# Front of a streaming encoder step: two more feature shifts summed by VectorE, late rows scaled by GpSimd and ScalarE, two jobs one place later

## The chip, the core and the metric

The kernel runs on one core of one Trainium2 chip. A core has TensorE (matrix products, PE in the profile, with PEld for its weight loads), VectorE (DVE), ScalarE (ACT), GpSimd (POOL) and SyncE (SP), which here issues nearly all transfers. Each engine works through its own queue in order, and engines wait for each other by semaphores. The metric is the device time of one execution in microseconds (us), lower is better.

## The reference

One layer of a hybrid encoder for 1024 prompt frames and 32 sample frames. The change lies in the first lines, the modulated norm and the input projection:

```python
mod = jax.nn.silu(c) @ w_ada + b_ada
sh1, sc1, gt1, sh2, sc2, gt2 = jnp.split(mod[:, None, :], 6, axis=-1)

h = rmsnorm(x, g_mix) * (1 + sc1) + sh1
u = h @ w_in
qa, ka, va, qm, km, vm, om, ip, fp, ga, gm = jnp.split(u, _split_points(), axis=-1)
```

`c` has one row for the prompt and one for the sample, so every feature has two scales and two shifts. After it come band attention over `qa, ka, va`, a matrix memory over `qm, km, vm`, gates, an output projection, and a SwiGLU network. All inputs are float32.

## The kernel before

**Layout.** Activations lie transposed: 1024 features in eight groups of 128 partitions ("features 0 to 7", index `k` or `j`), and 1056 token columns (1024 prompt, then 32 sample). The columns are worked in three tiles of 352. `CUT` is 704: tiles 0 and 1 are the *early* columns, tile 2 the *late* ones, and only the late tile has sample columns (its last 32).

**Precision.** A float32 product is made of three passes: high half of the weights by high half of the activations, low by high, high by low (`PASSES`). For each feature ScalarE writes the high half of `h` (`high_h`), and VectorE the low half (`low_h`).

**Order.** Engines PE, ACT, DVE and POOL run exactly in the order in which the code records their instructions. `first_units` is the opening of the kernel, written out by hand:

1. `load_ada(n)` fetches the halves of the modulation weights in order; `n = 2j` is the scale of feature `j`, `n = 2j + 1` its shift. `ada_sums(j, part, pt)` makes both on TensorE with eight products of 128x128 each, and `ada_done` turns them into `s1` and `sh1` on ScalarE. For feature 7 the shift is not made so: its weights lie with the 1024 inputs along a row, and `shift_sum` has VectorE multiply them with a broadcast copy of silu(c) (`silb`) and add up, once for the prompt (`c` = 0) and once for the sample (`c` = 1).
2. Squares of the early columns are summed, `token_roots` and `powers` (GpSimd) make the inverse roots, `spread` has TensorE transpose them over all partitions, and ScalarE copies them to `RB`.
3. `scaled_x` multiplies the columns by scale and root, `high_h` adds the shift. TensorE takes the early columns of the first key, value and query blocks: `products(k, q)` is pass `q` of feature `k`, six matmuls. The loop over `k` from 1 to 7 prepares feature `k + 2` on VectorE and ScalarE beside it. Within it the squares of the late columns are made, summed on TensorE (`token_sums`, at `k` = 3), rooted, spread (at `k` = 4), and from `k` = 5 on `late_h` prepares the late columns, one step of one feature at a time: `scaled_x(k)`, `high_h(k - 1)`, `low_h(k - 2)`.
4. After `k` = 7 ScalarE and VectorE empty the early results (`put_k`, `put_v`, `put_q`), while TensorE runs the 48 late products into the bank `psS`.

In the late columns the prompt part (320 columns) and the sample part (32) go different ways before the change: VectorE scales and subtracts the 320, GpSimd the 32.

**Behind the opening.** `unit` is the general product of a block and a tile; while it runs, it takes one job at a time out of `side.later`: transposes of values (`v_tail`, TensorE L694), the split of cached keys (`cache_keys`, ScalarE L769, VectorE L771) and of cached values (`cache_values`, VectorE L684 and L685). Attention then starts: VectorE L828 (scores and their maximum), ScalarE L829, TensorE L841 (transposes), ScalarE L848 and VectorE L853 (their two halves), TensorE L873.

## Time and profile before

| | |
|---|---|
| median of three runs | 1589.97 us (1589.28 to 1590.21) |
| profiled execution: its own time | 1588.91 us |
| its span, first to last instruction | 1587.2 us |
| granted TensorE clock, mean | 0.998 |
| busy: PE, PEld, DVE, ACT, POOL | 99%, 98%, 70%, 50%, 26% |
| end of the opening (last late product) | 70.7 us after the start |

The profiled execution takes 1.7 us more than its span, and 1.06 us less than the median. In rows of the timeline the first number is the start in us after the span's start, the second the duration of the row's instructions together; then come engine, line, operation, the tiles written and read, the shape and the count. The bracket tells how long the engine sat idle before it and what ended that. In rows of waits stand the total, the number of times and the longest.

### The profile page before, as it was taken

Reading aid. Unit: us, or ns where it says so; the run is one execution under the profiler, and the core shown is the slowest. Engines: PE = TensorE matmul, PEld = TensorE weight load, DVE = VectorE, ACT = ScalarE, POOL = GpSimd, SP = SyncE. Lnnn points to the kernel's source line nnn. Section 1 sums busy time; section 2 is a strip of 40 time slices with the busy share of each in tenths; the row PEclk is TensorE's granted clock in tenths of the full one; section 3 lists DMA queues with packets and bytes.
Section 4 is the critical chain, followed back from the end, with each engine's and each line's share of the span. In section 5 each row is a group of like instructions: output and inputs, shape, how many; then the busy total and the mean of one; then the engine's idle time right before and its main releaser. Section 6 shows DMA issues by size and latency. Waiting matters only on the chain.

```text
span 1587.2 us, 27275 instructions
## 1 busy us (share of the span) xinstructions
PE 1564.9 (99%) x10181; PEld 1547.8 (98%) x10181; DVE 1107.6 (70%) x2282; ACT 788.5 (50%) x1742; POOL 420.5 (26%) x438
## 2 busy tenths in 40 slices
PE   8999999999999999999999999999999999999997
PEld 8999999999999999999999999999999999999997
DVE  3865655556767845446655699898888986799755
ACT  4765554544555545444434656544545444545443
POOL 0433343442222410000012100665665750000000
PEclk9999999999999999999999999999999999999999
DMA  9422233243132423584353312223222227427444
GB/s 374 138 66 82 88 104 99 92 133 105 42 91 74 86 82 104 115 288 162 108 156 113 94 55 67 82 73 102 68 89 87 68 87 251 137 80 252 129 136 156
DMA packets 176481, 187.08 MB, mean 118 GB/s; under 512 B 11766, under 2 KB 141466, under 8 KB 176222
## 3 DMA queue, kind: packets, MB, share of 16 engines
q1 hardware_dynamic: 173686, 183.50, 36.7%
q10 hardware_dynamic: 2664, 1.85, 0.4%
q8 instruction: 80, 1.31, 0.4%
q14 instruction: 51, 0.42, 0.1%
HBM read 151.15 MB, written 34.17 MB: 117 GB/s over the span
## 4 chain that ended last, share of the span: by engine, by line
PE 92%; DVE 3%; ACT 2%; issue 2%; POOL 1%; DMA 0%; ACTq 0%; POOLq 0%; DVEq 0%
PE mm L418 41%; PE psb L1889 18%; PE mm L1889 11%; PE psb L2271 3%; PE mm L968 3%; PE mm L2271 2%; PE psV L873 2%; PE psb L2135 2%; PE psS L814 2%; PE mm L329 2%; PE psT L841 1%; PE mm L2135 1%; PE psV L1202 1%; PE psT L1204 1%; PE psT L1199 1%
## 5 line engine op out<-in xcount | busy, mean ns | idle before, releaser
L418 PE MATMUL mm<-s,wsp 128*128 128x352 f32 x4104 | 686.9, 324 | 0.1
L418 PEld LDWEIGHTS mm<-s,wsp 128*128 128x128 f32 x4104 | 657.1, 188 | 1.8 <-issue 0.4
L381 DVE TENSOR_TENSOR wsp<-wraw,wsp 128x512 fp32r<-128x512 f32 (+1 forms) x280 | 235.6, 859 | 113.7 <-ACT wsp L380 111.9
L1889 PE MATMUL psb<-s,wsp 128*128 128x352 f32 x1611 | 271.7, 322 | 1.5 <-DVE wsp L381 0.8
L380 ACT ACTIVATE wsp<-wraw 128x512 fp32r<-128x512 f32 x336 | 199.6, 617 | 141.5 <-PE psb L1889 43.8
L1889 PEld LDWEIGHTS psb<-s,wsp 128*128 128x128 f32 x1611 | 260.5, 188 | 2.1 <-DVE wsp L381 1.1
L1889 PE MATMUL mm<-s,wsp 128*128 128x352 f32 x933 | 159.3, 322 | 0.0
L1889 PEld LDWEIGHTS mm<-s,wsp 128*128 128x128 f32 x933 | 151.2, 188 | 0.5 <-DVE wsp L381 0.5
L834 POOL TENSOR_SCALAR st<-st,mx 128x640 f32<-128x640 f32 (+5 forms) x72 | 53.3, 740 | 183.6 <-DVE mx L833 165.6
L1295 DVE CUSTOM_DVE_ANT_0 junk<-wa,t 128x512 bf16<-128x512 f32 x128 | 94.8, 741 | 3.4 <-DMA wa<-in_w_mod_dram 2.3
L381 POOL TENSOR_TENSOR wsp<-wraw,wsp 128x512 fp32r<-128x512 f32 x56 | 74.9, 1358 | 52.6 <-ACT wsp L380 50.3
L828 DVE CUSTOM_DVE_ANT_0 st<-psS,bias 128x640 f32<-128x640 f32 (+5 forms) x72 | 44.5, 618 | 57.5 <-PE psS L814 43.5
L829 ACT ACTIVATE st<-st,mx 128x640 f32<-128x640 f32 (+5 forms) x72 | 47.9, 666 | 64.1 <-DVE mx L828 63.9
L1836 POOL TENSOR_TENSOR t<-t,sl 128x352 f32<-128x352 f32 x19 | 18.4, 967 | 212.7 <-ACT sl L1834 212.7
L848 ACT ACTIVATE pT<-psT 128x640 fp32r<-128x640 f32 (+3 forms) x80 | 38.6, 493 | 64.5 <-PE psT L841 50.1
L2244 POOL TENSOR_TENSOR fst<-fst,mhalf 128x6 f32<-128x6 f32 x1 | 2.3, 2312 | 221.1 <-DVE fst L2243 221.1
L853 DVE TENSOR_TENSOR pT<-psT,pT 128x640 fp32r<-128x640 f32 (+3 forms) x80 | 44.0, 558 | 21.5 <-ACT pT L848 21.4
L1508 POOL TENSOR_TENSOR wraw<-wraw,raw 128x512 f32<-128x512 f32 x33 | 55.8, 1704 | 0.9
L968 PE MATMUL mm<-s,s 128*128 128x264 f32 (+3 forms) x432 | 54.5, 283 | 0.0
L2271 PE MATMUL psb<-s,wsp 128*128 128x352 f32 x330 | 54.2, 324 | 0.0
L2271 PEld LDWEIGHTS psb<-s,wsp 128*128 128x128 f32 x330 | 53.1, 188 | 0.1
L968 PEld LDWEIGHTS mm<-s,s 128*128 128x128 f32 (+1 forms) x432 | 51.9, 179 | 0.5
(376 smaller groups left out, 2460.6 us busy)
## 6 DMA issues: line engine op xcount, KB each, us to landing
wraw<-in_w_in_dram SPq DMA_DIRECT2D x37, 512.0 KB, 3.7
wraw<-in_w_gate_up_dram SPq DMA_DIRECT2D x33, 512.0 KB, 3.9
wa<-in_w_mod_dram SPq DMA_DIRECT2D x64, 256.0 KB, 2.8
wraw<-in_w_down_dram SPq DMA_DIRECT2D x32, 512.0 KB, 4.3
a_d<-t SPq DMA_DIRECT2D x22, 528.0 KB, 2.8
g_d<-t SPq DMA_DIRECT2D x16, 528.0 KB, 3.4
t<-g_d SPq DMA_DIRECT2D x16, 528.0 KB, 4.8
s<-in_w_ada_dram SPq DMA_DIRECT2D x16, 512.0 KB, 8.0
```

Source lines behind the costliest of these rows:

```text
L380: act.activation(dst[:, 0], src, AF.Copy)
L381: eng.tensor_tensor(dst[:, 1], src, f(dst[:, 0]), op=ALU.subtract)
L418: pe.matmul(pt[:, :hi - lo], wt[(w0 + k) // 4][:, a, (w0 + k) % 4], xt[k][:, b, lo:hi], start=(k == 0 and q == 0), stop=(k == n - 1 and q ...
L828: dve.tensor_tensor_reduce(so, sv, bi, -1.0, 3.0e38, ALU.add, ALU.min, mx[:n, 1:2])
L829: act.activation(st[:n, :w], st[:n, :w], AF.Exp, bias=mx[:n, 1:2], scale=-1.0, accum_out=mx[:n, 2:3])
L834: pool.tensor_scalar(st[:n, :w], st[:n, :w], mx[:n, 3:4], 1.0, op0=ALU.mult, op1=ALU.mult)
L968: pe.matmul(pt[:n, :wd], hs[k][:, a, i * P:i * P + n], whl[b][:, k, :wd], start=(k == 0 and q == 0), stop=(k == KD - 1 and q == 2))
L1295: dve.tensor_tensor_reduce(junk, wa, crow[:, c], 1.0, 0.0, ALU.mult, ALU.add, at)
L1508: self.eng.tensor_tensor(a(dst), a(x), a(y), op=op)
L1889: pe.matmul(acc, wt[:, a, k], x[k][:, b], start=(start and not onto and k == 0 and q == 0), stop=(stop and k == 3 and q == 2), skip_group_ ...
L2135: pe.matmul(acc, wt[k // 4][:, u, k % 4], piece_of[k, i][:, v], start=(k == 0 and q == 0), stop=(k == KP - 1 and q == 2))
L2271: pe.matmul(acc, wt[(k - k0) // 4][:, u, (k - k0) % 4], piece_of[k, 2][:, v], start=(k == 0 and q == 0), stop=(k == NF - 1 and q == 2))
```

## The change

- `load_ada(13)`, the shift weights of feature 6, is fetched behind `silb` instead of ahead of the late columns of x; the host lays the shift weights of feature 6 out as those of feature 7.
- `ada_sums(6, 1)` on TensorE is gone. VectorE makes the shifts of feature 6 with two calls of `shift_sum`, so there are four in the loop, at `k` = 2, 4, 5 and 6, behind the `late_h` steps of their `k`.
- `ada_sums(7, 0)` stands ahead of the first products instead of behind their first pass; both `ada_done` stand earlier on ScalarE.
- The power of the early roots is taken in two instructions of three columns instead of one of six.
- The late columns of a feature are one piece of 352 for GpSimd (times `RB`), two for ScalarE (320 and 32, with scale and shift of their part, then one copy of 352 to the high half), and one of 352 for VectorE (the low half).
- The spread of the late roots stands behind `products(4, 2)`, and `cache_values` one place later among the side jobs.

```diff
     def load_ada(n):
         j, i = divmod(n, 2)
-        if i == 0:
+        if j == len(was):
             was.append(slot([P, 2, D]))
...
     load_first(0)
-    load_ada(13)
     load_ada(14)
...
-    def powers(t0, t1):
-        x = roots[:, :, 3 * t0:3 * t1]
-        pool.tensor_tensor(x[:, 1], x[:, 0], mhalf[:, :3 * (t1 - t0)], op=ALU.pow)
+    def powers(t):
+        x = roots[:, :, 3 * t:3 * t + 3]
+        pool.tensor_tensor(x[:, 1], x[:, 0], mhalf[:, :3], op=ALU.pow)
...
     def scaled_x(j, lo, hi):
-        for c, a, b in col_segments(lo, hi):
-            x = xTs[j][:, a:b]
-            if c == 0:
-                dve.scalar_tensor_tensor(x, x, s1[:, 0, j:j + 1], RB[:, a:b], op0=ALU.mult, op1=ALU.mult)
-            else:
-                pool.tensor_tensor(x, x, RB[:, a:b], op=ALU.mult)
+        x = xTs[j][:, lo:hi]
+        if hi <= CUT:
+            dve.scalar_tensor_tensor(x, x, s1[:, 0, j:j + 1], RB[:, lo:hi], op0=ALU.mult, op1=ALU.mult)
+        else:
+            pool.tensor_tensor(x, x, RB[:, lo:hi], op=ALU.mult)
 
     def high_h(j, lo, hi):
         if lo == 0:
             hs.append(slot([P, 2, T], F32R))
+        x, h = xTs[j][:, lo:hi], hs[j][:, 0, lo:hi]
+        if hi <= CUT:
+            act.activation(h, x, AF.Identity, bias=sh1[:, 0, j:j + 1])
+            return
         for c, a, b in col_segments(lo, hi):
-            x, h = xTs[j][:, a:b], hs[j][:, 0, a:b]
-            if c == 0:
-                act.activation(h, x, AF.Identity, bias=sh1[:, 0, j:j + 1])
-            else:
-                act.activation(x, x, AF.Identity, scale=s1[:, 1, j:j + 1], bias=sh1[:, 1, j:j + 1])
-                act.activation(h, x, AF.Copy)
+            o = xTs[j][:, a:b]
+            act.activation(o, o, AF.Identity, scale=s1[:, c, j:j + 1], bias=sh1[:, c, j:j + 1])
+        act.activation(h, x, AF.Copy)
 
     def low_h(j, lo, hi):
-        for c, a, b in col_segments(lo, hi):
-            x, o, h = xTs[j][:, a:b], hs[j][:, 1, a:b], f(hs[j][:, 0, a:b])
-            if c == 0:
-                dve.scalar_tensor_tensor(o, x, sh1[:, 0, j:j + 1], h, op0=ALU.add, op1=ALU.subtract)
-            else:
-                pool.tensor_tensor(o, x, h, op=ALU.subtract)
+        x, o, h = xTs[j][:, lo:hi], hs[j][:, 1, lo:hi], f(hs[j][:, 0, lo:hi])
+        if hi <= CUT:
+            dve.scalar_tensor_tensor(o, x, sh1[:, 0, j:j + 1], h, op0=ALU.add, op1=ALU.subtract)
+        else:
+            dve.tensor_tensor(o, x, h, op=ALU.subtract)
...
         sp.dma_start(silb, bass.AP(sil_d.tensor, sil_d.offset, [[0, P], [D, 2], [1, D]]))
+        load_ada(13)
         load_ada(15)
...
         spread(1)
-        ada_sums(6, 1, pt)
+        ada_done(6, pt)
+        ada_sums(7, 0, psS)
         for t in range(2):
             scaled_x(0, *early[t])
             high_h(0, *early[t])
-        ada_done(6, pt)
+        ada_done(7, psS)
...
             for i in range(3):
                 product(0, i, 0, t)
-        ada_sums(7, 0, psS)
         scaled_x(1, 0, CUT)
...
-            if k in (3, 4):
-                shift_sum(7, k - 3, silb)
+            for i in {5: (0, 1, 2), 6: (3, 4), 7: (5, 6)}.get(k, ()):
+                late_h(i)
+            for j, c in {2: [(6, 0)], 4: [(7, 0)], 5: [(6, 1)], 6: [(7, 1)]}.get(k, ()):
+                shift_sum(j, c, silb)
+            products(k, 2)
             if k == 4:
                 for i, n in enumerate((P, P, NT - 2 * P)):
                     pe.transpose(tok[:, i * P:i * P + n], roots[:n, 1, 6 + i:7 + i].to_broadcast([n, P]), ident[:n, :n])
                 act.activation(RB[:, late[0]:late[1]], tok[:, :NT], AF.Copy)
-            for i in {5: (0, 1, 2), 6: (3, 4), 7: (5, 6)}.get(k, ()):
-                late_h(i)
-            products(k, 2)
...
-                side.later += [lambda: cache_keys(early_loads[0]), nothing, lambda: cache_values(early_loads[0])]
+                side.later += [lambda: cache_keys(early_loads[0]), nothing, nothing, lambda: cache_values(early_loads[0])]
```

**VectorE, middle of the opening.** Before, between the weight splits of `k` = 2 and the low half of feature 5 (`s_46`). L351 is `scaled_x`, L370 `low_h`, L319 and L320 `token_roots` of the late columns, L336 and L337 `shift_sum`; `s_17` holds the weights of feature 7:

```order
L443 TENSOR_TENSOR s_35_340<-wraw_8_104,s_35_340 128x512
L351 SCALAR_TENSOR_TENSOR s_4_100<-s_4_100,s1_151,t_18_147 128x704
L370 SCALAR_TENSOR_TENSOR s_45_449<-s_4_100,sh1_150,s_45_449 128x704
L319 TENSOR_SCALAR roots_89<-psS_21_155 128x2
L320 TENSOR_SCALAR roots_89<-psS_21_155 96x1
L336 ISA s_17_138,shs_152<-s_17_138,s_23_183 128x1024
L336 ISA shs_152 128x1
L337 TENSOR_TENSOR sh1_150<-shs_152,cols_91 128x1
L351 SCALAR_TENSOR_TENSOR s_5_101<-s_5_101,s1_151,t_18_147 128x704
L370 SCALAR_TENSOR_TENSOR s_46_481<-s_4_100,sh1_150,s_46_481 128x704
```

The same stretch now, where `s_16` holds the weights of feature 6, and all lines of the file have moved up by one or two:

```order
L441 TENSOR_TENSOR s_35_341<-wraw_8_104,s_35_341 128x512
L335 ISA s_16_132,shs_151<-s_16_132,s_23_182 128x1024
L335 ISA shs_151 128x1
L336 TENSOR_TENSOR sh1_149<-shs_151,cols_91 128x1
L349 SCALAR_TENSOR_TENSOR s_4_100<-s_4_100,s1_150,t_18_146 128x704
L368 SCALAR_TENSOR_TENSOR s_45_441<-s_4_100,sh1_149,s_45_441 128x704
L318 TENSOR_SCALAR roots_89<-psS_21_154 128x2
L319 TENSOR_SCALAR roots_89<-psS_21_154 96x1
L349 SCALAR_TENSOR_TENSOR s_5_101<-s_5_101,s1_150,t_18_146 128x704
L368 SCALAR_TENSOR_TENSOR s_46_475<-s_4_100,sh1_149,s_46_475 128x704
```

A shift sum has come to stand ahead of `scaled_x(5)`, `low_h(4)` and the late roots; the one behind the roots is now behind `low_h(5)`.

**VectorE, end of the loop.** After the change, from the low half of feature 6 (`s_53`) to the third late low half; L370 is now `low_h` of late columns:

```order
L368 SCALAR_TENSOR_TENSOR s_53_516<-s_5_101,sh1_149,s_53_516 128x704
L370 TENSOR_TENSOR s_38_366<-s_2_98,s_38_366 128x352
L335 ISA s_16_132,shs_151<-s_16_132,s_23_182 128x1024
L335 ISA shs_151 128x1
L336 TENSOR_TENSOR sh1_149<-shs_151,cols_91 128x1
L368 SCALAR_TENSOR_TENSOR s_54_544<-s_5_101,sh1_149,s_54_544 128x704
L370 TENSOR_TENSOR s_42_382<-s_2_98,s_42_382 128x352
L370 TENSOR_TENSOR s_43_392<-s_3_99,s_43_392 128x352
```

Before, three scalings of late columns and one late low half stood between the low halves of features 6 and 7; now one late low half and a shift sum do.

**VectorE, first attention scores.** Before, around `cache_values` (L684, L685), in `side.later`:

```order
L833 RECIPROCAL mx_88_903<-mx_88_903 128x1
L624 TENSOR_TENSOR s_78_853<-mm_80_859,s_78_853 64x352 x2
L684 CAST s_85_893<-t_50_501 128x8x64
L685 TENSOR_TENSOR s_85_893<-t_50_501,s_85_893 128x8x64
L828 ISA st_93_941,mx_94_942<-psS_92_940,bias_51_504 128x384
L828 ISA mx_94_942 128x1
L853 TENSOR_TENSOR pT_91_937<-psT_90_936,pT_91_937 128x128
```

And now:

```order
L623 TENSOR_TENSOR s_78_833<-mm_80_839,s_78_833 64x352 x2
L827 ISA st_93_919,mx_94_920<-psS_92_918,bias_51_498 128x384
L827 ISA mx_94_920 128x1
L852 TENSOR_TENSOR pT_91_915<-psT_90_914,pT_91_915 128x128
L832 RECIPROCAL mx_94_920<-mx_94_920 128x1
L683 CAST s_85_873<-t_50_495 128x8x64
L684 TENSOR_TENSOR s_85_873<-t_50_495,s_85_873 128x8x64
```

The split of the cached values has moved behind the third scores and the low half of the first transposes.

More of the change, by code (lines that the diff above doesn't have):

```diff
@@ L279, in hybrid_stream_step @@
     s1 = cp.tile([P, 2, KD], F32, name="s1")
-    shs = cp.tile([P, 2], F32, name="shs")
+    shs = cp.tile([P, 2, 2], F32, name="shs")
     gm1 = cols[:, R_GMIX:R_GMIX + KD]
@@ L333, in shift_sum @@
     def shift_sum(j, c, silb):
-        at = shs[:, c:c + 1]
+        at = shs[:, j % 2, c:c + 1]
         dve.tensor_tensor_reduce(was[j][:, 0], was[j][:, 1], silb[:, c], 1.0, 0.0, ALU.mult, ALU.add, at)
@@ L340, in ada_done @@
         act.activation(s1[:, :, j], pt[:, :2], AF.Identity, scale=gm1[:, j:j + 1], bias=gb1[:, j:j + 1])
-        if j == KD - 1:
+        if j >= KD - 2:
             return
@@ L466, in first_units @@
             token_roots(i, hi - lo, 3 * DH * i, DH)
-        powers(0, 2)
+        for i in range(2):
+            powers(i)
         pt = mmt()
@@ L519, in first_units @@
         high_h(2, 0, CUT)
-        ada_done(7, psS)
         products(0, 2)
@@ L552, in first_units @@
                 token_roots(2, NT, NT, 32)
-                powers(2, 3)
+                powers(2)
                 W.loaded = W.split_n = 3
@@ L2325 @@
             a = _np.asarray(inputs["w_ada"])[0, :, :2 * D].reshape(KD, P, 2, KD, P)
-            last = a[:, :, 0, -1].reshape(D, P).T
+            last = a[:, :, 0, -2:].transpose(2, 3, 0, 1).reshape(2, P, D)
             a = a.transpose(2, 3, 1, 0, 4)[::-1].reshape(2, KD, P, D).copy()
-            a[1, -1] = last
+            a[1, -2:] = last
         else:
```

## Prediction

> **What bounds the kernel.** I read the page's busy shares, then the stretches, then TensorE's waits, then the timeline of the first 92 us engine by engine.
>
> ```profile
> PE 1564.9 (99%) x10181; PEld 1547.8 (98%) x10181; DVE 1107.6 (70%) x2282; ACT 788.5 (50%) x1742; POOL 420.5 (26%) x438
> 29.30:70.60 41.30, 40.37 (x270) 39.22 (x270) 35.12 (x63) 28.52 (x67) 13.61 (x22) 1.00 0.59 207
> 91.10:1587.00 1495.90, 1482.11 (x9604) 1466.95 (x9604) 1052.84 (x2183) 735.35 (x1625) 396.82 (x395) 1.00 0.36 111
> PE psT L841 <- DVE pT L853: 2.3, 3, 1.8
> PE psS L562 <- POOL roots L324: 0.6, 1, 0.6
> ```
>
> A stretch's row gives its bounds and length, then the busy time of PE, PEld, DVE, ACT and POOL, the clock and DMA. TensorE is busy nearly without a gap, so the time is its work plus its waits. A change in the first 92 us is worth what it moves TensorE there; the remaining 1495.9 us hold 1482.1 us of TensorE work that isn't touched, and I let the shift pass through them unchanged. In the opening TensorE waits little, but VectorE is busy 35.1 of 41.3 us, and it is VectorE that gets new work.
>
> **Step 1, first products.**
>
> ```profile
> 31.15 1.28 DVE L443 TENSOR_TENSOR wsp<-wraw,wsp 128x512 fp32r<-128x512 f32 x2
> 31.38 1.65 POOL L324 TENSOR_TENSOR roots<-roots,mhalf 128x6 f32<-128x6 f32 x1 [29.86 <-DVE roots L320]
> 32.35 0.68 DVE L443 TENSOR_TENSOR s<-wraw,s 128x512 fp32r<-128x512 f32 x1
> 33.08 0.96 PE L230 MATMUL mm<-ident,roots 128*128 128x128 f32 x6 [0.27 <-POOL roots L324]
> 33.97 2.05 PE L329 MATMUL mm<-csil,s 128*128 128x128 f32 x16
> 36.62 0.19 PEld L492 LDWEIGHTS mm<-s,wsp 128*128 128x128 f32 x1 [0.40 <-ACT sh L343]
> 37.20 1.94 PE L329 MATMUL psS<-csil,s 128*128 128x128 f32 x16
> 38.91 0.57 PE L492 MATMUL mm<-s,wsp 128*128 128x352 f32 x2
> 1579.05 0.56 POOL L2212 TENSOR_TENSOR est<-est,mhalf 128x1 f32<-128x1 f32 x1
> 51.00 1.77 POOL L324 TENSOR_TENSOR roots<-roots,mhalf 128x3 f32<-128x3 f32 x1 [17.97 <-DVE roots L320]
> ```
>
> TensorE does a feature sum twice here, at 33.97 and 37.20. The change drops `ada_sums(6, 1)` and puts `ada_sums(7, 0)` in its place, so the second block of some 1.8 us goes (38.91 - 37.05, where its first weight load can go). Against it: the early roots take two powers in a row. A power costs 0.56 us (1 column, nothing beside it) to 1.77 (3 columns, beside VectorE). I take 0.8 for three columns, plus the wait for a running VectorE instruction: the first ends at 32.6, the second, held by the third L443 to 33.0, at 33.85 instead of 33.03. The second spread, and the sum behind it, come 0.4 us later; but the 0.40 us that the products lost to `ada_done` (row at 36.62) go, since that now stands ahead. The first pass ends at 37.2 as before; then -1.8 us. With 1.77 for each power it would be -0.9. On SyncE's queue the shift weights of feature 6 go past the late x, three half weights and `silb`, which all go one place up. Nothing reads these shift weights before 48.6, so their delay of a few us is covered by more than ten; if it weren't, VectorE would stand there.
>
> **Step 2, middle of the opening.**
>
> ```profile
> 39.19 0.35 ACT L340 ACTIVATE s<-psS,gb,cols 128x2 f32<-128x2 f32 x1 [0.42 <-PE psS L329]
> 43.19 0.69 DVE L443 TENSOR_TENSOR wsp<-wraw,wsp 128x512 fp32r<-128x512 f32 x1 [1.05 <-ACT wsp L439]
> 45.52 2.34 DVE L297 TENSOR_TENSOR t<-t,s 128x352 f32<-128x352 f32 x4
> 48.61 0.70 PE L309 MATMUL psS<-ones,t 128*128 128x32 f32 x6
> 49.84 0.95 DVE L370 SCALAR_TENSOR_TENSOR s<-s,sh,s 128x704 fp32r<-128x704 f32 x1
> 50.84 1.21 DVE L336 CUSTOM_DVE_ANT_0 s<-s,s 128x1024 f32<-128x1024 f32 x1
> 52.17 0.94 DVE L351 SCALAR_TENSOR_TENSOR s<-s,s,t 128x704 f32<-128x704 f32 x1
> 52.83 0.52 PE L562 MATMUL psS<-ident,roots 128*128 128x128 f32 x3 [0.55 <-POOL roots L324]
> 62.83 7.84 PE L492 MATMUL psS<-s,wsp 128*128 128x352 f32 x48
> ```
>
> A matmul of 352 columns takes 7.84/48 = 0.163 us, a pass 0.98. The late squares are added up at 47.86 (45.52 + 2.34), so VectorE has no slack for TensorE's 1.8. The `ada_done` of feature 7 no longer stands ahead of ScalarE's squares (39.19), for whose end VectorE waited 1.05 us at 43.19; I give VectorE 0.45 of it, between 0 and 0.67 that ScalarE gains (from the end of `high_h(2)` to the squares). The sums can start at 47.4, TensorE is there at 46.8 (48.61 - 1.8) and waits 0.55. Then a shift sum (50.84 to 52.17, so 1.33 us) stands ahead of `scaled_x(5)` and `low_h(4)`: that ends at 49.84 + 0.95 - 0.45 + 1.33, about 51.7, where pass 2 of feature 4 wants it at 50.9. Wait 0.8. The late roots also come 0.9 later; their power, held by `scaled_x(6)`, ends at 53.5, some 0.65 after TensorE has finished pass 2 and stands before the transposes. Before, pass 2 came behind the transposes (52.83 + 0.35 + 0.98 = 54.15 for the start of feature 5); now it lies ahead of them, and feature 5 starts at 53.8. Of 1.8 us, 0.35 is left.
>
> **Step 3, the late rows.**
>
> ```profile
> 58.59 0.55 ACT L361 ACTIVATE s<-s,sh 128x320 fp32r<-128x320 f32 x1
> 59.04 0.40 ACT L363 ACTIVATE s<-s,sh,s 128x32 f32<-128x32 f32 x1
> 59.47 0.23 ACT L364 ACTIVATE s<-s 128x32 fp32r<-128x32 f32 x1
> 59.61 0.55 ACT L361 ACTIVATE s<-s,sh 128x320 fp32r<-128x320 f32 x1
> 72.10 0.47 ACT L622 ACTIVATE kf<-psS 128x352 f32<-128x352 f32 x1
> 65.73 1.87 ACT L619 ACTIVATE s<-mm 64x352 fp32r<-64x352 f32 x4
> 79.93 2.58 POOL L381 TENSOR_TENSOR wsp<-wraw,wsp 128x512 fp32r<-128x512 f32 x2
> 80.09 1.26 DVE L685 TENSOR_TENSOR vst<-stg,vst 32x128 fp32r<-32x128 f32 x1
> 858.20 0.95 POOL L1836 TENSOR_TENSOR t<-t,sl 128x352 f32<-128x352 f32 x1 [2.90 <-ACT sl L1834]
> 858.61 1.69 DVE L381 TENSOR_TENSOR wsp<-wraw,wsp 128x512 fp32r<-128x512 f32 x2 [1.15 <-ACT wsp L380]
> ```
>
> ScalarE: a feature takes 1.02 us (58.59 to 59.61). Of it 0.45 and 0.43 stay; the copy grows from 32 to 352 columns and holds the engine about 0.37 (0.47 less the 0.10 by which neighbours overlap), so 1.25: 8 x 0.23 = +1.85 us.
>
> GpSimd: eight scalings of 352 columns, 0.95 each. They don't run freely beside VectorE. Two L381 that take 1.28 alone (like those at 31.15) took 1.69 beside the GpSimd scaling at 858.20; and a 32-row subtraction lasted 1.26 at 80.09, until the first of two GpSimd subtractions was through. So instructions of both that read two tiles of SBUF take turns, and GpSimd holds about 0.8 us of its 0.95. Turn by turn, with 0.87 us for a 704-column VectorE instruction (49.84, less the overlap), 0.5 for a late low half, 1.33 for a shift sum: GpSimd starts at 54.8, behind a shift sum; `scaled_x(7)` ends at 56.5, `low_h(6)` at 58.2, the first late low half (its high half is out at 58.7) at 59.4, the shift sum (6, 1) at 61.3, and `low_h(7)` at 62.9, with five scalings let in between. TensorE wants it at 61.6 (53.8 and eight passes) and waits 1.35. Late products start at 63.9 instead of 62.83; those of the fourth feature wait 0.45 more for their low half, behind the shift sum (7, 1). Together +1.8, so TensorE is at +1.45 when they end, near 72.1. ScalarE's late rows start 0.35 sooner, but the last waits 0.7 for that shift sum: with 1.85 that makes +2.2, and `put_k` starts near 68 instead of 65.73.
>
> [...]
>
> **Step 4, to the first transposes.**
>
> ```profile
> 73.69 0.47 ACT L660 ACTIVATE t<-psS 128x352 f32<-128x352 f32 x1
> 74.33 0.60 PE L694 MATMUL mm<-ident,t 128*128 128x128 f32 x4
> 88.99 0.43 DVE L684 CAST s<-t 128x512 fp32r<-128x512 f32 x1
> 90.18 0.56 DVE L828 CUSTOM_DVE_ANT_0 st<-psS,bias 128x384 f32<-128x384 f32 x1
> 91.09 0.41 PE L841 MATMUL psT<-ident,st 128*128 128x128 f32 x2 [1.76 <-DVE pT L853]
> 92.81 1.06 DVE L624 TENSOR_TENSOR s<-mm,s 64x352 fp32r<-64x352 f32 x2 [1.13 <-ACT kf L622]
> ```
>
> The value transposes at 74.33 read what L660 wrote up to 74.16: ScalarE has 0.2 us of slack there, so its +2.2 becomes +2.1, for both engines. From there to 91.09 the chain runs over ScalarE, GpSimd and VectorE, with TensorE ahead of it by 1.76 us. On this chain the cast and split of the cached values (88.99 to 90.18) go from in front of L828: -1.19. They land in the 1.13 us for which VectorE waits ahead of 92.81, at no cost; without that gap they would cost at most the same 1.19. TensorE resumes at 91.09 + 2.1 - 1.19 = 92.0.
>
> **Sum.** -1.8 (feature sum) + 1.45 (step 2: 0.55 + 0.8 + 0.65 of new waits, less the 0.55 at 52.83) + 1.8 (step 3) + 0.65 (ScalarE's lateness beyond TensorE's, 2.1 - 1.45) - 1.2 (cached values) = +0.9 us. The profiled execution was 1588.91, so 1589.8; it lies 1.06 under the median, so against 1589.97 I say **1590.9**.
>
> **Rivals.**
> - *GpSimd and VectorE don't disturb each other here.* VectorE rows of 704 columns before (0.95 at 49.84) keep their length, but only beside GpSimd work of 32 columns. Then `low_h(7)` is in time, and ScalarE's late rows end 0.3 to 1.1 later (1.85, less an earlier start of `high_h(7)`): at 91 us -0.9 to -0.1, so 1589.1 to 1589.9.
> - *TensorE, not ScalarE, sets the pace from 71 to 91.* TensorE keeps its 0.35, and of the 1.76 wait all but 0.1 goes: -2.0, 1588. Against it speak the 0.2 us of slack at 74. A gain over 0.2% needs all of this and no late wait at all.
> - *Slower: GpSimd keeps its turn.* If its next scaling, already queued, wins each time, all eight run first, 54.8 to 62.4. `scaled_x(7)` then ends at 63.4, `high_h(7)` 0.9 later, and ScalarE's eight rows of 1.25 at 74: +8 against 65.73, -1.2 for the cached values, so +6.8 and 1596.8. Each scaling in a row ahead of `scaled_x(7)` costs 0.9; from four on the whole is slower by over 0.2%. The row at 80.09 speaks against it: VectorE got in after one. [...]
>
> **Numbers.** Step sums as told 0.62; no disturbance 0.22; TensorE's pace 0.10; GpSimd first 0.06. A change under 0.2% (3.2 us) can't be told here from none. All but the last case, and 0.03 of the third, lie inside it; of the first I leave 0.01 either side. So faster 0.04, same 0.89, slower 0.07. The first case by itself goes from -0.4 (a power at 0.56, all 0.67 of ScalarE's gain to VectorE) to +2.2 (GpSimd holding all of its 0.95, powers of 1.77 where VectorE's backlog doesn't hide them): 1589.6 to 1592.2. With the second, the nearer half of the third, and 0.6 us by which single runs differ, the range is 1588.4 to 1592.4.
>
> **What would show it.** TensorE: no feature sum between the first two passes; pass 1 starting near 37.2; waits of about 0.55, 0.8 and 0.65 before the late sums, pass 2 of feature 4 and the transposes; one of over 1 us at pass 2 of feature 7. VectorE rows of 704 columns near 1.5 us between 55 and 63. ScalarE's first `put_k` row near 68 instead of 65.73. The wait for L853 under 0.8 us instead of 1.76. I am wrong if GpSimd's eight scalings run without a gap, if `low_h(7)` is done before 61.6, or if ScalarE's lateness is gone by 74.

## The result, and the profile after

The changed kernel takes **1592.99 us** (median; 1591.08 to 1594.41), the kernel before beside it 1589.14 (1588.76 to 1590.21): a ratio of **1.0024, 95% interval 1.0016 to 1.0031**. That is 3.85 us more, by over 0.2%; 0.9 was predicted, and the time lies above the predicted range. The profiled execution took 1593.66 us, its span is 1591.9.

Two stretches of the trace of the changed kernel (columns as before the change):

```profile
29.30:70.60 41.30, 36.02 (x224) 34.02 (x223) 36.07 (x57) 27.89 (x58) 15.80 (x13) 0.96 0.57 205
94.83:1591.80 1496.97, 1482.68 (x9604) 1466.92 (x9604) 1055.01 (x2185) 734.15 (x1625) 394.83 (x395) 1.00 0.36 111
```

In the opening TensorE is busy 36.0 us where it was busy 40.4, and its mean clock there is 0.96 instead of 1.00. The last row starts where TensorE resumes at the first transposes, at 94.83 instead of 91.09: the 9604 matmuls behind it take 1.07 us more in this one execution. So 3.74 us of loss stand at that point. Timeline of the first half of the opening, GpSimd and TensorE:

```profile
31.23 2.56 POOL L323 TENSOR_TENSOR roots<-roots,mhalf 128x3 f32<-128x3 f32 x2 [29.72 <-DVE roots L316]
...
33.85 0.63 PE L230 MATMUL mm<-ident,roots 128*128 128x128 f32 x3 [0.65 <-POOL roots L323]
34.41 2.05 PE L328 MATMUL psS<-csil,s 128*128 128x128 f32 x16
...
47.46 0.80 PE L308 MATMUL psS<-ones,t 128*128 128x32 f32 x6 [0.42 <-DVE t L296]
51.72 0.58 PE L493 MATMUL mm<-s,wsp 128*128 128x352 f32 x2 [0.48 <-DVE s L368]
53.42 0.52 PE L564 MATMUL psS<-ident,roots 128*128 128x128 f32 x3 [0.47 <-POOL roots L323]
```

The last three brackets are the new waits of step 2, 0.42, 0.48 and 0.47 us. Now the late rows, on GpSimd, VectorE and ScalarE:

```profile
54.52 9.80 POOL L351 TENSOR_TENSOR s<-s,t 128x352 f32<-128x352 f32 x8 [1.15 <-ACT t L565]
...
54.70 0.78 DVE L336 TENSOR_TENSOR sh<-shs,cols 128x1 f32<-128x1 f32 x1
55.40 1.71 DVE L349 SCALAR_TENSOR_TENSOR s<-s,s,t 128x704 f32<-128x704 f32 x1
57.04 1.63 DVE L368 SCALAR_TENSOR_TENSOR s<-s,sh,s 128x704 fp32r<-128x704 f32 x1
59.57 1.19 DVE L370 TENSOR_TENSOR s<-s,s 128x352 fp32r<-128x352 f32 x1 [0.90 <-POOL s L351]
60.69 1.97 DVE L335 CUSTOM_DVE_ANT_0 s<-s,s 128x1024 f32<-128x1024 f32 x1
...
62.69 0.76 DVE L336 TENSOR_TENSOR sh<-shs,cols 128x1 f32<-128x1 f32 x1
63.38 1.69 DVE L368 SCALAR_TENSOR_TENSOR s<-s,sh,s 128x704 fp32r<-128x704 f32 x1
...
57.99 0.94 ACT L362 ACTIVATE s<-s,sh,s 128x320 f32<-128x320 f32 x2
58.97 0.50 ACT L363 ACTIVATE s<-s 128x352 fp32r<-128x352 f32 x1
59.37 0.95 ACT L362 ACTIVATE s<-s,sh,s 128x320 f32<-128x320 f32 x2
...
69.03 1.86 ACT L618 ACTIVATE s<-mm 64x352 fp32r<-64x352 f32 x4
```

GpSimd's eight scalings run without a gap, 9.80 / 8 = 1.22 us each. VectorE's rows of 704 columns take 1.6 to 1.7 us instead of 0.95, its one-column addition 0.78 instead of 0.16. `low_h(7)`, the row at 63.38, is done at 65.07. ScalarE takes 1.38 us for a feature (57.99 to 59.37), and `put_k` starts at 69.03. What TensorE makes of it, as timeline rows and then as short stretches; the row of ScalarE between them is its first one on the late products:

```profile
65.13 0.59 PE L493 MATMUL mm<-s,wsp 128*128 128x352 f32 x2 [3.26 <-DVE s L368]
66.20 9.40 PE L493 MATMUL psS<-s,wsp 128*128 128x352 f32 x48
...
75.63 0.93 ACT L618 ACTIVATE s<-psS 64x352 fp32r<-64x352 f32 x2 [1.21 <-PE psS L493]
...
62.91:66.32 3.41, 1.19 (x7) 1.20 (x8) 3.41 (x5) 3.31 (x9) 2.10 (x3) 1.00 0.24 89
66.32:69.74 3.42, 3.42 (x14) 3.42 (x13) 3.19 (x8) 3.35 (x9) 1.25 (x2) 0.50 0.18 65
69.74:73.15 3.41, 3.41 (x23) 3.41 (x22) 2.59 (x6) 3.31 (x10) 0.43 (x1) 1.00 0.00 0
```

TensorE waits 3.26 us for `low_h(7)`. Then its granted clock is 0.50 for 3.4 us: 14 matmuls, where the stretch of the same length behind it has 23. The 48 late products take 9.40 us instead of 7.84 and end 4.93 us later than before (75.60 for 70.67), and ScalarE, though late itself, waits 1.21 us for them. Last, the first transposes, and the cached values behind them:

```profile
94.83 0.41 PE L840 MATMUL psT<-ident,st 128*128 128x128 f32 x2 [0.63 <-DVE pT L852]
95.77 0.96 DVE L684 TENSOR_TENSOR s<-t,s 128x512 fp32r<-128x512 f32 x1
```

The wait for the low half is 0.63 us where it was 1.76.

| point | predicted | after |
|---|---|---|
| start of feature 5 on TensorE | 53.8 | 53.7 |
| `low_h(7)` done | 62.9 | 65.07 |
| TensorE's wait for it | 1.35 | 3.26 |
| late products done | 72.1 | 75.60 |
| `put_k` starts on ScalarE | 68 | 69.03 |
| TensorE resumes at the first transposes | 92.0 | 94.83 |

### The profile page after: what moved, and what is told of

Same layout as the page of the kernel before. It is cut to its first block, busy times and chain, and to the rows that moved or that the text cites. A ratio compares the mean times of both kernels' runs of the same rounds, so it can differ in the third digit from the quotient of the medians.

```text
span 1591.9 us, 27224 instructions
## 1 busy us (share of the span) xinstructions
PE 1565.9 (98%) x10165; PEld 1547.0 (97%) x10165; DVE 1112.3 (70%) x2280; ACT 790.0 (50%) x1741; POOL 421.8 (26%) x431
## 3 DMA queue, kind: packets, MB, share of 16 engines
q10 hardware_dynamic: 2664, 1.85, 0.4%
## 4 chain that ended last, share of the span: by engine, by line
PE 89%; DVE 4%; ACT 3%; DMA 2%; issue 1%; POOL 1%; SPq 0%; ACTq 0%; DVEq 0%; POOLq 0%
PE mm L416 39%; PE psb L1888 18%; PE mm L1888 11%; PE psb L2270 3%; PE mm L967 3%; PE mm L2270 2%; PE psV L872 2%; PE psb L2134 2%; PE psS L813 1%; PE psT L840 1%; DMA s<-in_w_ada_dram 1%; PE mm L2134 1%; PE psS L493 1%; DVE st L827 1%; PE psV L1201 1%
## 5 line engine op out<-in xcount | busy, mean ns | idle before, releaser
L379 POOL TENSOR_TENSOR wsp<-wraw,wsp 128x512 fp32r<-128x512 f32 x56 | 74.5, 1349 | 53.7 <-ACT wsp L378 50.2
L828 ACT ACTIVATE st<-st,mx 128x640 f32<-128x640 f32 (+5 forms) x72 | 47.9, 666 | 63.1 <-DVE mx L827 62.9
```

Source lines behind the costliest of these rows:

```text
L379: eng.tensor_tensor(dst[:, 1], src, f(dst[:, 0]), op=ALU.subtract)
L828: act.activation(st[:n, :w], st[:n, :w], AF.Exp, bias=mx[:n, 1:2], scale=-1.0, accum_out=mx[:n, 2:3])
```

## The experiments

Each ran in five rounds beside the kernel before, which took 1589.08 us (first four), 1588.91 (next four), 1588.94 (next two) and 1589.26 (last). Differences are against that. Intervals of the ratios are about 0.0009 to either side, that is 1.4 us, so the time of one run settles no half microsecond; the rows of its trace carry the finer readings. A run has eleven executions, that of the late rows alone six.

**The wait without the idle time.** The changed kernel with 18 matmuls more where TensorE waits; their results are overwritten.

```diff
             products(k, 1)
...
+            if k == 7:
+                for _ in range(18):
+                    pe.matmul(psS[:, :NT], W.blocks[0][3][0][:, 0, 0], hs[0][:, 0, :NT], start=True, stop=True)
             products(k, 2)
```

> The changed kernel with 18 more matmuls of 352 columns on TensorE (2.9 us, into a part of psS that the late products overwrite) ahead of pass 2 of feature 7, where TensorE stood 3.26 us. Theory A (the wait itself lowers the granted clock, 0.58 for 4 us, which cost the late products 9.40 - 7.84 = 1.56 us): with TensorE kept busy the clock stays 1.00, the 48 late products take 7.84, and as ScalarE was 1.2 us ahead of TensorE behind them, the time is 1.2 us less, about 1591.8. Rival B (the clock fell by chance or for another reason): the clock falls again, 1593.0 as before.

Measured 1591.46 us (+2.38), ratio 1.0013 (1.0005 to 1.0022). TensorE's timeline in this run:

```profile
61.66 3.06 PE L563 MATMUL psS<-s,wsp 128*128 128x352 f32 x18
65.12 0.59 PE L493 MATMUL mm<-s,wsp 128*128 128x352 f32 x2 [0.41 <-DVE s L368]
66.19 7.85 PE L493 MATMUL psS<-s,wsp 128*128 128x352 f32 x48
...
93.30 0.41 PE L843 MATMUL psT<-ident,st 128*128 128x128 f32 x2 [0.66 <-DVE pT L855]
```

Pass 2 of feature 7 starts at the same 65.12, but TensorE was idle for only 0.41 us ahead of it, and the late products take 7.85 us. TensorE resumes at 93.30, 1.53 sooner than in the changed kernel, and the medians differ by 1.5 us. That part of the loss was clock, not waiting. The executions of the changed kernel itself agree: ten with a mean clock of 0.996 or 0.997 took 1592.52 to 1594.41 us, three with 0.998 or 0.999 took 1591.08 to 1592.11. All eleven of this run are at 0.998.

**The shift sums later.** The sums (6, 1) and (7, 1) one place later, so that none stands ahead of `low_h(7)`:

```diff
-            for j, c in {2: [(6, 0)], 4: [(7, 0)], 5: [(6, 1)], 6: [(7, 1)]}.get(k, ()):
+            for j, c in {2: [(6, 0)], 4: [(7, 0)], 6: [(6, 1)], 7: [(7, 1)]}.get(k, ()):
```

> The changed kernel with the two shift sums of the sample one step of the loop later (k = 6 and 7 instead of 5 and 6), so that low_h(7) stands ahead of both. Theory A (VectorE and GpSimd take turns, one scaling of 0.8 to 1.2 us for each VectorE instruction of two SBUF tiles): low_h(7) loses the 1.97 + 0.76 us of the shift sum and ends at 62.4 instead of 65.07; the wait at pass 2 falls from 3.26 to about 0.6 and the clock stays 1.00; ScalarE's rows stay 1.38 each and now set the end, so the time is 1.2 us less, 1591.8. Rival C (the added shift sums alone make VectorE late, GpSimd costs nothing): low_h(7) ends by 61, no wait, VectorE rows of 704 columns at 0.95, and 1589.5.

Measured 1591.71 us (+2.63), ratio 1.0016 (1.0008 to 1.0025). TensorE's waits and ScalarE's first `put_k` row:

```profile
62.41 0.59 PE L493 MATMUL mm<-s,wsp 128*128 128x352 f32 x2 [0.48 <-DVE s L368]
...
69.17 1.87 ACT L618 ACTIVATE s<-mm 64x352 fp32r<-64x352 f32 x4
...
77.65 0.55 PE L693 MATMUL mm<-ident,t 128*128 128x128 f32 x3 [2.17 <-ACT t L659]
```

The 3.26 us wait is gone, and the time is that of the run before, as far as these intervals tell. TensorE only waits later: `put_k` starts as late as ever, and the value transposes wait 2.17 us for ScalarE's L659. So the long wait cost nothing but its clock; ScalarE's lateness lay under it.

**Late rows as before.** The changed kernel with `scaled_x`, `high_h` and `low_h` of the kernel before:

```diff
-            pool.tensor_tensor(x, x, RB[:, lo:hi], op=ALU.mult)
...
+                dve.scalar_tensor_tensor(x, x, s1[:, 0, j:j + 1], RB[:, a:b], op0=ALU.mult, op1=ALU.mult)
+            else:
+                pool.tensor_tensor(x, x, RB[:, a:b], op=ALU.mult)
```

> The changed kernel with scaled_x, high_h and low_h of before: late columns scaled by VectorE (320) and GpSimd (32) again; the four shift sums, the order of the opening and the cached values as changed. Theory A: VectorE rows back at 0.95 and 0.54, low_h(7) done at 60.7, no wait at pass 2 of feature 7, clock 1.00, ScalarE rows of 1.02; but the two added shift sums (1.33 each) make the last late rows about 1.5 late; with -1.2 from the cached values 1589 to 1590. Rival C (the sums make VectorE late): a wait of over 2 us at pass 2, clock below 1.00 after it, 1592 or more.

Measured 1589.71 us (+0.63), ratio 1.0004 (0.9995 to 1.0013): the late rows carry 3.2 of the 3.85 us. VectorE's `low_h(7)`, two late rows and `put_k` of ScalarE, and TensorE's wait for the value transposes:

```profile
59.52 0.96 DVE L369 SCALAR_TENSOR_TENSOR s<-s,sh,s 128x704 fp32r<-128x704 f32 x1
...
60.98 0.56 ACT L360 ACTIVATE s<-s,sh 128x320 fp32r<-128x320 f32 x1 [0.88 <-DVE s L350]
64.24 0.57 ACT L360 ACTIVATE s<-s,sh 128x320 fp32r<-128x320 f32 x1 [1.10 <-DVE s L350]
67.32 1.87 ACT L619 ACTIVATE s<-mm 64x352 fp32r<-64x352 f32 x4
...
75.81 0.55 PE L694 MATMUL mm<-ident,t 128*128 128x128 f32 x3 [1.72 <-ACT t L660]
```

`low_h(7)` is done at 60.5 and TensorE doesn't wait for it. `put_k` is still 1.6 us later than the 65.73 of before: ScalarE's old rows wait 0.88 and 1.10 us for scalings (L350) that stand behind the shift sums on VectorE.

**Late rows alone.** The kernel before with nothing changed but those three functions.

```diff
-            if c == 0:
-                dve.scalar_tensor_tensor(x, x, s1[:, 0, j:j + 1], RB[:, a:b], op0=ALU.mult, op1=ALU.mult)
...
+            pool.tensor_tensor(x, x, RB[:, lo:hi], op=ALU.mult)
```

> The kernel before with only the late rows of the change (GpSimd scales 352 columns, ScalarE adds and copies, VectorE subtracts 352); two shift sums, order and cached values as before. Theory A: GpSimd's eight scalings and VectorE take turns, VectorE rows of 704 columns at 1.6 to 1.7 us; TensorE waits 0 to 1 us at pass 2 of feature 7, clock 1.00; ScalarE rows of 1.38 instead of 1.02 make its put_k 3 us later, which comes through to 91 us: 1591.5 to 1592.5. Rival C: VectorE rows at 0.95, at most 1 us of ScalarE's lateness, 1589 to 1590.

Measured 1593.92 us (+4.84), ratio 1.0029 (1.0018 to 1.0041), over a microsecond more than expected. TensorE's wait for the value transposes, and two stretches, around it and behind it:

```profile
77.77 0.84 PE L693 MATMUL mm<-ident,t 128*128 128x128 f32 x3 [2.17 <-ACT t L659]
...
74.48:77.89 3.41, 1.24 (x9) 0.95 (x8) 2.16 (x4) 3.27 (x8) 2.43 (x4) 1.00 0.24 82
77.89:81.31 3.42, 3.42 (x13) 3.42 (x14) 1.38 (x2) 1.73 (x4) 1.41 (x2) 0.50 0.27 50
```

It is the 2.17 us wait of the second run again, but here the clock falls after it, to 0.50 for 3.4 us. The expectation had the mechanism and not this price.

**Cached values alone**, in the kernel before:

```diff
-                side.later += [lambda: cache_keys(early_loads[0]), nothing, lambda: cache_values(early_loads[0])]
+                side.later += [lambda: cache_keys(early_loads[0]), nothing, nothing, lambda: cache_values(early_loads[0])]
```

> The kernel before, with the split of the cached values one place later and nothing else changed. Theory A (step 4 of the prediction was right: the cast and split of 1.19 us leave VectorE's chain to the first transposes and land in a gap): TensorE's wait for the low half of the first transposes falls from 1.76 us to about 0.6, the transposes start near 89.9 instead of 91.09, and the time is near 1588.0 where before takes 1589.1. Rival B (the split only moves to another place of the same chain and is paid there): the transposes come sooner, but the time stays at 1589.1 within 0.3.

Measured 1588.23 us (-0.68), ratio 0.9997 (0.9988 to 1.0006). TensorE's first and second transposes with the split between them on VectorE:

```profile
90.12 0.41 PE L841 MATMUL psT<-ident,st 128*128 128x128 f32 x2 [0.58 <-DVE pT L853]
91.07 0.95 DVE L685 TENSOR_TENSOR s<-t,s 128x512 fp32r<-128x512 f32 x1
94.31 0.52 PE L841 MATMUL psT<-ident,st 128*128 128x128 f32 x3 [0.32 <-DVE pT L853]
```

The wait falls from 1.76 to 0.58, as step 4 said. But the split takes 0.95 us in its new place instead of 0.69, the gap it fills is 1.13 us for 1.4 us of work, and the next low half is late by 0.32. Of 1.2 us some 0.3 are given back.

**Cached values and the late transposes**, in the kernel before: beside the edit above, the spread of the late roots stands behind `products(4, 2)`, as in the change.

```diff
+            for i in {5: (0, 1, 2), 6: (3, 4), 7: (5, 6)}.get(k, ()):
+                late_h(i)
+            products(k, 2)
             if k == 4:
...
-            products(k, 2)
```

> The kernel before, with the cached values one place later and the transposes of the late roots behind the third pass of feature 4. Theory A: the 0.55 us wait for the late power goes, but from 71 to 91 ScalarE sets the pace and its late rows start no sooner, so at most 0.4 us come on top of the run with the cached values alone: 1587.6 to 1588.0. Rival B (TensorE sets the pace there): the whole 0.55 comes through, 1587.4 or less. With the run that has the old late rows (1589.7) it also prices the four shift sums of VectorE in the place of two and of a feature sum: 1589.7 less 1587.8, a loss of 1.9 us where the prediction had a loss of about 0.4 by then.

Measured 1588.30 us (-0.61), ratio 0.9996 (0.9987 to 1.0005), above the 1587.6 to 1588.0 that was expected. The wait of 0.55 us ahead of the transposes is gone, and this one has come:

```profile
74.19 0.55 PE L694 MATMUL mm<-ident,t 128*128 128x128 f32 x3 [0.33 <-ACT t L660]
```

So ScalarE sets the pace there already in the kernel before, within 0.2 us, and a gain on TensorE alone buys nothing that shows in the time. Against the run with the old late rows, 1.2 us (0.63 + 0.61) are left as the price of the shift sums on VectorE and the new order of the opening together, with a feature sum less on TensorE.

**Shift sums and order of the opening alone**: the run with the old late rows, with the cached values at their old place too.

```diff
-                side.later += [lambda: cache_keys(early_loads[0]), nothing, nothing, lambda: cache_values(early_loads[0])]
+                side.later += [lambda: cache_keys(early_loads[0]), nothing, lambda: cache_values(early_loads[0])]
```

> The changed kernel with the late rows of the kernel before and the cached values at their old place: only the shift sums, the order of the opening and the place of the late transposes are changed. Theory A (the parts add up): 1.2 us over the run that has the cached values later as well (1589.7), so 1590.9. Rival B (with ScalarE's lateness the cached values no longer lie on the path): 1589.7.

Measured 1590.65 us (+1.74), ratio 1.0012 (1.0003 to 1.0021), 1.1 us over the run with the old late rows: the parts add up. The wait for the low half stands at its old length:

```profile
92.98 0.41 PE L841 MATMUL psT<-ident,st 128*128 128x128 f32 x2 [1.68 <-DVE pT L853]
```

**Scaling on VectorE.** The changed kernel, without GpSimd in the late rows:

```diff
-            pool.tensor_tensor(x, x, RB[:, lo:hi], op=ALU.mult)
+            dve.tensor_tensor(x, x, RB[:, lo:hi], op=ALU.mult)
```

> The changed kernel, with the scaling of the late rows moved from GpSimd to VectorE: eight instructions of 352 columns more for VectorE, near 0.54 us each, and none for GpSimd. ScalarE's longer late rows (1.38 us per feature) stay. Theory A (the loss comes from GpSimd and VectorE taking turns): although VectorE gets 4 us of work more, its 704-column rows are back at 0.95 us, its one-column addition at 0.16, low_h(7) ends before 61.5 instead of 65.07, TensorE waits under 0.3 us there and keeps its clock, put_k starts near 68.0, and the time is 1590.2 to 1590.8 where the changed kernel takes 1593.0. Rival B (VectorE simply has too much work there, or ScalarE's longer rows carry the loss): low_h(7) ends at 64 or later, or put_k at 69, and the time is 1591.7 to 1593.

Measured 1591.86 us (+2.95; 1590.83 to 1592.19), ratio 1.0016 (1.0008 to 1.0025). VectorE's `low_h(7)`, one of ScalarE's late rows, its `put_k`, TensorE's wait:

```profile
60.32 0.94 DVE L368 SCALAR_TENSOR_TENSOR s<-s,sh,s 128x704 fp32r<-128x704 f32 x1
...
61.74 0.96 ACT L362 ACTIVATE s<-s,sh,s 128x320 f32<-128x320 f32 x2 [0.46 <-DVE s L351]
...
68.98 1.87 ACT L618 ACTIVATE s<-mm 64x352 fp32r<-64x352 f32 x4
...
77.45 0.55 PE L693 MATMUL mm<-ident,t 128*128 128x128 f32 x3 [2.16 <-ACT t L659]
```

Every VectorE row is back at its own length (0.94 to 0.95 us at 704 columns, 0.16 for the one-column addition), and `low_h(7)` is done at 61.26, 3.8 us sooner, though VectorE has eight scalings more. Yet `put_k` starts as late as in the changed kernel. Theory A was right on VectorE and wrong on the time, where rival B held. ScalarE's late rows start 1.0 us sooner than in the changed kernel (57.02), but twice they wait for scalings that now stand behind the shift sums on VectorE (0.46 us here, 0.20 at 64.82), which costs about 0.9 from start to start. The longer rows alone would keep `put_k` at 68.1 (57.02 + 8 x 1.38, an estimate); with these waits it is back at 69.

**ScalarE's rows short.** The changed kernel with the second run's order of the shift sums, and ScalarE writing straight into the high half. The copy is left out, and the low half is made from rows without scale and shift, so only the time of this run means something:

```diff
-            o = xTs[j][:, a:b]
-            act.activation(o, o, AF.Identity, scale=s1[:, c, j:j + 1], bias=sh1[:, c, j:j + 1])
-        act.activation(h, x, AF.Copy)
+            act.activation(hs[j][:, 0, a:b], xTs[j][:, a:b], AF.Identity, scale=s1[:, c, j:j + 1], bias=sh1[:, c, j:j + 1])
```

> The changed kernel with the shift sums (6, 1) and (7, 1) one place later (the run that took 1591.7 us without TensorE's long wait), and ScalarE writing the scaled and shifted late rows straight into the high half. That leaves out the copy of 352 columns, and the low half of the late columns is then made from rows without scale and shift. GpSimd's eight scalings and their turns with VectorE stay. Theory A (ScalarE's longer late rows carry the loss): a feature costs ScalarE about 0.98 us instead of 1.38, put_k starts near 66.2 instead of 69.2, TensorE's wait of 2.17 us for L659 goes, and the time is 1588.6 to 1589.6. Rival B (the turns between GpSimd and VectorE carry it): the time stays at 1591.4 to 1592.

Measured 1590.85 us (+1.91; 1590.21 to 1591.9), ratio 1.0013 (1.0004 to 1.0022): between the two theories. ScalarE's last late rows and `put_k`:

```profile
65.71 0.96 ACT L361 ACTIVATE s<-s,sh,s 128x32 fp32r<-128x32 f32 x2 [1.81 <-DVE sh L336]
67.93 0.41 ACT L361 ACTIVATE s<-s,sh,s 128x32 fp32r<-128x32 f32 x1 [1.26 <-DVE sh L336]
68.25 1.87 ACT L616 ACTIVATE s<-mm 64x352 fp32r<-64x352 f32 x4
```

ScalarE is ahead now and waits 1.81 and 1.26 us for the shift sums of the sample, which VectorE, held up by GpSimd, finishes only at 65.7 and 67.9. `put_k` gains 0.9 us of the 3 expected. So there are two causes side by side, and each alone keeps `put_k` at 68 to 69.

**The 2 us wait filled.** The run with the scaling on VectorE, with twelve matmuls in TensorE's wait for L659:

```diff
             c0 = (g * 4 + i) * P
+            if (hp, g, i) == (0, 1, 1):
+                for _ in range(12):
+                    pe.matmul(pt[:, P:P + NT], hs[0][:, 0, :P], hs[0][:, 0, :NT], start=True, stop=True)
             pe.transpose(pt[:, i * P:(i + 1) * P], vf[:, c0:c0 + P], ident)
```

> The run that scaled the late rows on VectorE took 1590.8 to 1591.0 us in four executions with a granted clock of 0.998 and 1591.7 to 1592.2 in seven with 0.997 (median 1591.86). Here it gets twelve matmuls of 352 columns, some 2 us, between the first and the second value transpose, where TensorE waited 2.16 us for L659; their results are overwritten by the transposes. Theory A (in the seven the clock fell after that wait): all executions are near 1590.9, 1590.6 to 1591.4, at 0.998. Rival B (the clock falls elsewhere, or the 1 us has another cause): both groups stay, median 1591.6 to 1592.

Measured 1591.01 us (+2.07; 1590.88 to 1591.53), ratio 1.0013 (1.0004 to 1.0021). The wait in TensorE's timeline:

```profile
77.19 0.55 PE L696 MATMUL mm<-ident,t 128*128 128x128 f32 x3 [0.24 <-ACT t L659]
```

All eleven executions have a mean clock of 0.998, and the slower group of the unfilled run has gone: in the unfilled run the seven executions at 0.997 took about 1 us more than the four at 0.998, and with the 2.16 us wait filled none is at 0.997.

**Both causes gone**: the run with ScalarE's short rows, with the scaling on VectorE as well. It leaves out the same work as that run.

```diff
-            pool.tensor_tensor(x, x, RB[:, lo:hi], op=ALU.mult)
+            dve.tensor_tensor(x, x, RB[:, lo:hi], op=ALU.mult)
```

> The run in which ScalarE writes the late rows straight into the high half (the copy and the scale and shift of the low half are left out, 1590.85 us), with the scaling by the roots moved from GpSimd to VectorE as well. Theory A (two causes in parallel, either of which alone holds put_k back: ScalarE's longer rows, and VectorE's shift sums pushed back by GpSimd's turns): with both gone ScalarE no longer waits more than 1 us for the shift sum (7, 1), put_k starts at 66.3 to 67.3 instead of 68.25, TensorE's wait for L659 is near 1 us, and the time is 1588.9 to 1589.8. Rival B (the shift sums themselves, four of them on VectorE, hold the rows whoever scales): put_k stays at 68 or later and the time at 1590.5 to 1591.

Measured 1588.89 us (-0.37; 1588.74 to 1589.34), ratio 0.9998 (0.9989 to 1.0007). ScalarE's `put_k` and TensorE's wait:

```profile
66.73 1.87 ACT L616 ACTIVATE s<-mm 64x352 fp32r<-64x352 f32 x4
...
75.21 0.55 PE L691 MATMUL mm<-ident,t 128*128 128x128 f32 x3 [1.14 <-ACT t L657]
```

Four runs with the same opening and no long wait at feature 7 make a square (the one with 1.38 us rows and the scaling on VectorE has the shift sums where the change put them, the others have the later order; the medians of the three slower ones hold some executions with the clock at 0.997):

| | ScalarE rows 1.38 us | ScalarE rows short |
|---|---|---|
| scaling on GpSimd | `put_k` 69.17, +2.63 us | 68.25, +1.91 |
| scaling on VectorE | 68.98, +2.95 (+2.07 with the wait filled) | 66.73, -0.37 |

Taking away one cause moves `put_k` by 0.2 or 0.9 us, taking away both by 2.4. The 0.2 isn't the price of the turns alone, since the scalings on VectorE brought ScalarE waits of their own.

## Why the prediction was wrong, step by step

- **Step 1 was right.** There is no feature sum between the first passes, the second power cost TensorE 0.65 us (33.85), and pass 1 starts at 37.2.
- **Step 2 was right.** Waits of 0.42, 0.48 and 0.47 stand where 0.55, 0.8 and 0.65 were expected, and feature 5 starts at 53.7. A lead of TensorE alone is worth nothing there, since ScalarE sets the pace behind it (the run with the late transposes).
- **Step 3 failed in its sizes.** TensorE's wait at feature 7 was put at 1.35 us and measured 3.26; ScalarE's eight late rows were put at +1.85 us and measured +2.9.

  *ScalarE's row*: the working had 1.25 us, it measured 1.38. The copy cost about what it said (0.40, from 58.97 to 59.37); the two scaled rows ahead of it take 0.98 from start to start (57.99 to 58.97) and not 0.45 + 0.43, and the 320-column one, which now reads a scale as well, 0.64 us instead of 0.55. Eight times 0.13 is 1.0 us, as much as `put_k` missed 68 by, but that these agree is luck: the rows started at 57.99 and not near 57.2 (0.35 sooner than before), and the last didn't wait the 0.7 us for the shift sum (7, 1), which was done at 67.28; the two cancel.

  *VectorE's turns*: each turn cost what it said, 0.6 to 0.8 us. That GpSimd holds all of its 0.95 us, the case at the upper end of the range, no run shows. The number of turns was short. The one-column addition behind a shift sum pays a whole turn too (0.78 and 0.76 us, for 0.16). The first made `scaled_x(7)` 0.6 late, and by that and its longer row ScalarE has the first late high half out at 59.47 (58.97 + 0.50) instead of 58.7; for it, and not for GpSimd, which the bracket names, the late low half waits until 59.57. That half pays 0.4 more than was counted, the second addition 0.6: 0.9 + 0.4 + 0.6 of the 2.2 us by which `low_h(7)` missed 62.9. The other 0.3 is a slip in the sum: with 0.8 a turn, 1.33 for the shift sum and 0.87 for the row, 59.4 leads to 63.2.

  The order was the expected one, turn by turn; GpSimd did run without a gap, which the prediction had put down as a sign against itself, but by longer instructions (1.22 us) and not by going first.
- **A term was missing: the clock.** It was put at nothing, without a reason given. The sum counted the wait at feature 7 by its length. The trace of before showed no drop after its one wait of 1.76 us, and the prediction carried none over to a longer one. The wait itself cost nothing beyond ScalarE's lateness (second run), the drop behind it 1.5 us (first run).
- **Step 4 was right in its mechanism, and too high by 0.1 to 0.5.** ScalarE's lateness does pass to both engines, and the cached values leave the chain. Alone they gave 0.68 us, and 1.1 between the runs with the old late rows, instead of 1.19; the 0.32 at the next low half went back.
- **The sum.** In the trace of the changed kernel TensorE is the late one at the end of the late products, by 4.93 us where 1.45 was predicted: 1.9 more for the wait and 1.56 for the clock. Less 1.2 for the cached values, that is the 3.74 at the first transposes. Without the clock TensorE would be 3.4 late, and ScalarE, at `put_k`, is 3.3 late; this is why the second run, without the wait, gained no more than the first, in which only the drop is gone. By the runs, from the kernel before to the changed one step by step, so that the parts add up by construction: cached values -0.7, late transposes 0, shift sums and order of the opening +1.2, late rows +1.75 (first run less the one with the old late rows), clock +1.5. The order matters: put first, on the kernel before, the late rows with the clock cost 4.84 and not 3.2.
- **The rivals.** That GpSimd and VectorE don't disturb each other is ruled out by the rows. That TensorE sets the pace from 71 to 91 is ruled out where the clock stays up (TensorE waits 2.17 us for ScalarE in the second run); in the changed kernel it came to hold, but with TensorE made late by its clock, and not with the gain that this rival forecast. That GpSimd runs all eight first did not happen: seven VectorE instructions got in beside the eight.

What stays open: why the profiled execution lost 1.07 us behind 94.83; it lies 0.7 above the median. Matmul by matmul against the trace of before, 0.2 of it goes at the second transposes and 0.4 and 0.5 at two waits of TensorE for VectorE's L1635, near 711 and 723 us, where the trace of before has none; what set these off isn't known. In the run with the scaling on VectorE the profiled execution was one of the four at 0.998; that the clock fell after the 2.16 us wait in the other seven is shown by the filling alone. What makes ScalarE's 320-column row 0.09 us longer can be told: in the run with the short rows it writes fp32r into another tile, as before the change, and still takes 0.66 us (the row at 63.24, against 0.55 before), so by these rows it is the scale that it now reads.

The cached values alone, or with the late transposes, are the only parts that gained, 0.6 to 0.7 us, and their intervals include no change.

## What to carry to other kernels

When work moves off a busy engine, look for the second engine that is as late as the first: here ScalarE's longer rows and VectorE's turns with GpSimd each held the same point, so removing either alone gained 0.7 us or less. Count GpSimd's cost to VectorE per VectorE instruction with two inputs in SBUF and not per column: beside GpSimd's scalings here the one-column addition lost 0.62 us (0.78 for 0.16), the 704-column row at 63.38 lost 0.74 (1.69 for 0.95). And price a long new wait of TensorE twice: once by its length, which later slack may hide, and once by the clock behind it. After the 3.26 us here it was 0.50 for 3.4 us, which came through almost whole (1.5 of 1.56 us); after a wait of 2.17 us it fell in one trace (the late rows alone) and stayed at 1.00 in another (the second run).

## What the hardware showed that had not been expected

- *Clock.* In the clock record of the changed kernel's trace 58.027 us at 1.00 lie ahead of the fall at 66.32, then 3.413 at 0.50, then 1515.518 at 1.00 up to the fall at the kernel's end; that of before has one stretch of 1570.131 at 1.00. These are 17, 1, 444 and 460 times 3.4133 us. Both falls in the opening, at 66.32 and with the late rows alone at 77.89, last 3.4 us at 0.50. In the 3.41 us ahead of them TensorE was busy for 1.19 and 1.24, so idle for 2.2 (62.91 and 74.48 in the rows above). In the profile of the run with ScalarE's short rows it was idle for 1.87 us of 3.41, and the clock stayed:

```profile
73.29:76.70 3.41, 1.54 (x10) 1.25 (x9) 2.30 (x4) 3.28 (x8) 2.42 (x4) 1.00 0.21 78
76.70:80.12 3.42, 3.20 (x20) 2.86 (x21) 1.38 (x2) 2.02 (x4) 1.55 (x2) 1.00 0.28 40
```

  It also stayed in the kernel before, with its wait of 1.76 us. The length of the wait alone does not settle it: with the late rows alone the clock fell after 2.17 us, and in the profiles of the second run and of the run with the scaling on VectorE it stayed at 1.00 after 2.17 and 2.16. The executions of the latter fall into two groups, four at 0.998 (1590.83 to 1591.03 us) and seven at 0.997 (1591.68 to 1592.19). What decides between them is not shown.
- *GpSimd beside VectorE.* GpSimd's scaling of 352 columns took 1.22 us, where a GpSimd row of that shape took 0.95 in the trace of before (858.20). Each VectorE instruction with two inputs in SBUF lost 0.6 to 0.8 beside it, from one column (0.78 us for 0.16) to 1024, custom reduction included (1.97 us for 1.21); the accumulator read at 62.58, which reads no tile, kept its 0.08. VectorE lost less than 0.95 us each time, and the two engines took turns one by one: seven such instructions beside eight scalings.
